# A hybrid decoder block: how its first modulation is loaded and summed, and where the next tokens' transposes stand

## The chip, the cores and the metric

One core of a Trainium2 chip runs the whole kernel in one launch. The metric is the device time of one execution in microseconds (us); less is better. TensorE multiplies matrices, VectorE, ScalarE and GpSimd do element-wise work, SyncE (SP) only issues transfers; each engine takes its instructions in the order of its own queue, and semaphores hold an instruction until what it needs is there.

## The reference

One transformer block over 2048 tokens of width 1024, in float32. Only the parts near the change are shown; the two mixers (a gated linear attention with four heads and a differential attention with four heads), the output projection and the squared-ReLU MLP follow.

```
ada = silu(c) @ ada_w + ada_b                 # c: (1, 1024), ada_w: (1024, 6 * 1024)
sh_a, sc_a, gt_a, sh_m, sc_m, gt_m = split(ada, 6)
h = rms_norm(x, pre_norm_mix) * (1 + sc_a) + sh_a
proj = h @ w_in                               # gla q, k, v, gate rank 16, out gate; diff q, k, v
g_log = log_sigmoid(g_lr @ gate_w + gate_b) / 16
y = concat(gla heads, diff heads) @ w_out
x = x + gt_a * rms_norm(y, post_norm_mix)
...                                           # the MLP, with sh_m, sc_m, gt_m
```

## The kernel before

Tokens go in four groups of 512 (`t` = 0 to 3); a contraction over 1024 is eight steps `k` of 128. Every float32 product is three products of a high and a low part (fp32r): high x high, high x low, low x high. The code is written with a framework that sets the order of each engine's queue itself, from priorities in the order of the program and from a model of when operands, buffers and PSUM banks are ready; so an instruction written later can stand earlier in a queue.

*The start.* `ada_cols(j)` (lines 352 to 370) forms one 1024-wide part of `ada`: eight blocks of ada_w (128 x 1024 each, 512 KB) are loaded into three buffers of tag `wraw`, VectorE multiplies each by a column of silu(c) and adds it to `acc`, and eight products with a column of ones sum `acc` over the partitions into columns. It is done for part 1 (the scale `sc_a`) and then for part 0 (the shift `sh_a`); `load_consts` stands after the first three blocks, and the loads of the first 512 tokens of x after three blocks of the shift. All of these transfers are issued by SP. The buffers `wraw` also hold the raw projection weights.

*A group of tokens.* `load_norm` (line 132) loads four tiles of x, ScalarE squares and sums them, and each is scaled by its inverse root. `modulate` (line 150) then takes eight steps: four transposes on TensorE (L155), scale and shift on ScalarE (L157), the high part on VectorE (L158), the low part on VectorE and GpSimd in turn (L160). The results `hThi`, `hTlo` have two buffers each.

*The gate.* `gate_scan` (line 507) multiplies the tokens by the rank-16 weights (16 products `lrps`, L513 and L514), copies the result out (L516), and for each half `j` makes one product with gate_w (`zps`, L519), an activation chain on ScalarE and a running sum on VectorE. `gates(t)` (line 531) turns this into the decay factors.

*The projections.* `gla_proj` (line 542) takes the weight blocks 2 and 3 with `proj_n` (tokens on the partitions, two PSUM banks of 48 products for each group of tokens, copied out at L553), then 4, 5, 0 and 1 with `proj_t`. The products `lrps`, `zps` and the projections share two PSUM banks of tag "A", the transposes of `modulate` two of tag "C". `gates(0)` is written before `gla_proj`; in it, `norm_in(1)` and `gates(1)` are written between the two groups of the first weight block. For groups 2 and 3, `norm_in(2)` and `gates(2)` are written among the last projections of the groups before, and the same call follows.

*The output projection.* `out_proj` (line 858) goes through the tiles of 128 tokens: it loads the mixed tile `mx` (1 MB, two buffers, in two pieces for the last four tiles) from DRAM, loads x, makes two banks of 24 products each (L873 to L875), and adds the normed result to x. It is a generator: `interleave` (line 945) runs its steps between those of the attention. A tile can only be taken when all heads of its tokens are finished.

Of the kernel before, what the change touches and what calls it, by code (L numbers as in the profile page):

```python
# [14 lines left out]
ALU = mybir.AluOpType  # L15
# [34 lines left out]
def tile_hybrid_block(  # L50
# [48 lines left out]
    def load_consts():  # L99
        nc.sync.dma_start(cols, ada_b)  # L100
        nc.sync.dma_start(prem[:, 0, :], pre_mix)
        nc.sync.dma_start(prem[:, 1, :], pre_mlp)
        nc.sync.dma_start(postm[:, 0, :], post_mix)
        nc.sync.dma_start(postm[:, 1, :], post_mlp)
        nc.sync.dma_start(gnc[:, 0:1], gla_norm)
        nc.sync.dma_start(gnc[:, 1:2], diff_norm)
        nc.sync.dma_start(gbc, gate_b)
        nc.sync.dma_start(ivf, inv_freq)
        nc.sync.dma_start(gw2[0:16], gate_w)
        nc.sync.dma_start(gw2[16:32], gate_w)  # L110
        nc.sync.dma_start(lamt, lams.partition_broadcast(P))

# [19 lines left out]
    def load_norm(src, xp, slots, on_act=False):  # L132

        xts = []
        ss = xp.tile([P, 4], F32, tag="nss", name="nss", bufs=2)
        for i in range(4):
            xt = xp.tile([P, D], F32, tag=slots[i][0], name="nx", bufs=slots[i][1])
            nc.sync.dma_start(xt, src[i])
            junk = xp.tile([P, D], BF16, tag="njunk", name="njunk", bufs=1)
            nc.scalar.activation(junk, xt, AF.Square, accum_out=ss[:, i:i + 1])  # L140
            xts.append(xt)
        r = rsqrt_col(xp, ss, 4, 1.0 / D, "nr")
        for i in range(4):
            if on_act:
                nc.scalar.activation(xts[i], xts[i], AF.Copy, scale=r[:, i:i + 1])
            else:
                nc.vector.tensor_scalar(xts[i], xts[i], r[:, i:i + 1], None, op0=ALU.mult)
        return xts

    def modulate(xts, a1, sh, hi, lo, tp, ttag, tb, pp, ptags):  # L150

        for k in range(NK):
            ps = pp.tile([P, 512], F32, tag=ptags[k % len(ptags)], name="ntr", bufs=2)
            for i in range(4):
                nc.tensor.transpose(ps[:, i * P:(i + 1) * P], xts[i][:, k * P:(k + 1) * P], ident)  # L155
            hf = tp.tile([P, 512], F32, tag=ttag, name="nhf", bufs=tb)
            nc.scalar.activation(hf, ps, AF.Identity, bias=sh[:, k:k + 1], scale=a1[:, k:k + 1])  # L157
            nc.vector.tensor_copy(hi[:, k, :], hf)  # L158
            eng = nc.gpsimd if k % 2 else nc.vector
            eng.tensor_tensor(lo[:, k, :], hf, hi[:, k, :].bitcast(F32), op=ALU.subtract)  # L160


# [148 lines left out]
    def ps_proj(name):  # L311
        return pp.tile([P, 512], F32, tag="A", name=name, bufs=2)
# [96 lines left out]

    def norm_in(t, xts=None, ptags="C"):  # L410
        hi = sb.tile([P, NK, 512], F32R, tag="hThi", name="hThi", bufs=2)
        lo = sb.tile([P, NK, 512], F32R, tag="hTlo", name="hTlo", bufs=2)
        xts = xts or load_x(t)
        modulate(xts, prem[:, 0, :], cols[:, 0:NK], hi, lo, sb, "tA", 8, pp, ptags)
        hT[t] = (hi, lo)

    def split_w(p, pool, nb, eng=nc.vector):
# [11 lines left out]

    sc_a = ada_cols(1)  # L430
    run(sc_a, 3)
    load_consts()
    run(sc_a)
    make_a1(0, 1)
    sh_a = ada_cols(0, sb.tile([P, 4, 256], F32, tag="whi", name="adacc", bufs=3).rearrange("p a b -> p (a b)"))
    run(sh_a, 3)
    xts = load_x(0)
    run(sh_a)
    norm_in(0, xts, "CBDCBDCB")

# [51 lines left out]

    def proj_n(w, t, i2):

        ps = ps_proj("projn")
        whi, wlo = w
        hi, lo = hT[t]
        for i in range(2):
            o = ps[:, i * 256:(i + 1) * 256]
            tk = slice((2 * i2 + i) * P, (2 * i2 + i + 1) * P)  # L500
            for k in range(NK):
                nc.tensor.matmul(o, hi[:, k, tk], whi[k], start=(k == 0), stop=False)  # L502
                nc.tensor.matmul(o, hi[:, k, tk], wlo[k], start=False, stop=False)  # L503
                nc.tensor.matmul(o, lo[:, k, tk], whi[k], start=False, stop=(k == NK - 1))
        return ps

    def gate_scan(t, consts, pool, ta):

        hi, lo = hT[t]
        lw1, lw2, rst = consts[0:3]  # L510
        ps = ps_proj("lrps")
# [3 lines left out]
        lrT = pool.tile([32, 512], F32, tag="lrT", name="lrT", bufs=1)  # L515
        nc.vector.tensor_copy(lrT, ps[0:32, :])  # L516
        for j in range(2):
            zp = ps_proj("zps")
# [11 lines left out]

    def gates(t):
        for j, b16 in gate_scan(t, glac, sg, tA):

# [7 lines left out]

    def gla_proj(ts2):
        for q in range(2):
            w = load_w(2 + q)
            run(rope, 1)
            for t in ts2:
                if q == 0 and t % 2:
                    norm_in(t)
                    gates(t)
                for i2 in range(2):  # L550
                    ps = proj_n(w, t, i2)
                    ev = tA("gvev", F32, (P, 2, 256))
                    nc.scalar.copy(ev.rearrange("p a b -> p (a b)"), ps)  # L553
                    nc.gpsimd.dma_start(gvS[t][:, 2 * i2:2 * i2 + 2, 256 * q:256 * q + 256], ev)
# [101 lines left out]
    def gla_any(tq, gn, gcon, masks):  # L656
# [8 lines left out]
        xts = load_norm([x[tq * 512 + i * P:tq * 512 + (i + 1) * P, :] for i in range(4)], gn, [("nx", 4)] * 4)  # L665
        modulate(xts, prem[:, 0, :], cols[:, 0:NK], hi, lo, gn, "nhf", 2, pp, "C")
        hT[tq] = (hi, lo)
        b16s = [b for _, b in gate_scan(tq, gcon, gn, ta)]
        qr, kr = [], []
# [115 lines left out]

    gates(0)
    gla_proj((0, 1))
    dp, ga = diff_proj((0, 1)), gla((0, 1))
# [3 lines left out]

    norm_in(2)
    run(dp, 1)
    gates(2)
    run(dp)
    run(ga)
    gla_proj((2, 3))
    dp, ga = diff_proj((2, 3)), gla((2, 3))
# [58 lines left out]
    def out_proj(tiles):  # L858

        for tk in tiles:  # L860
            assert all((tk // 4, h) in finished for h in range(NH))
            mx = sw.tile([P, 2 * NH, 2, P], F32R, tag="mx", name="mx", bufs=2)
            for ks in (slice(0, 7), slice(7, 8)) if tk >= 12 else (slice(0, 8),):
                nc.sync.dma_start(mx[:, ks].bitcast(F32), mixS[tk // 4][:, tk % 4, ks])
            xt = sw.tile([P, D], F32, tag="wx", name="wxt", bufs=3)
            nc.sync.dma_start(xt, x[tk * P:(tk + 1) * P, :])
            yps = []
            ss = sw.tile([P, 2], F32, tag="wss", name="wss", bufs=2)
            for b in range(2):
# [631 lines left out]
```

## Time and profile before

| | |
|---|---|
| time, median of 3 runs | 2626.18 us (2623.98 to 2628.01) |
| the profiled execution: its time, its span | 2620.44 us, 2618.7 us |
| TensorE busy | 2482.6 us, 95% of the span |
| VectorE, ScalarE, GpSimd busy | 1595.4, 1154.8, 435.5 us |
| mean granted TensorE clock | 0.982 of full speed |
| mean DMA rate | 188 GB/s |

The span runs from the first to the last instruction of one profiled execution. Busy shares are means over stages with different limits: what a stage can gain is read from its own stretch and from which wait ends last there. Matmuls are pipelined, so the time from one start to the next says more of their price than the duration of one.

### The profile page before, as it was taken

Reading aid. Unit: us, or ns where it says so; the run is one execution under the profiler, and the core shown is the slowest. Engines: PE = TensorE matmul, PEld = TensorE weight load, DVE = VectorE, ACT = ScalarE, POOL = GpSimd, SP = SyncE. Lnnn points to the kernel's source line nnn. Section 1 sums busy time; section 2 is a strip of 40 time slices with the busy share of each in tenths; the row PEclk is TensorE's granted clock in tenths of the full one; section 3 lists DMA queues with packets and bytes.
Section 4 is the critical chain, followed back from the end, with each engine's and each line's share of the span. In section 5 each row is a group of like instructions: output and inputs, shape, how many; then the busy total and the mean of one; then the engine's idle time right before and its main releaser. Section 6 shows DMA issues by size and latency. Waiting matters only on the chain.

```text
span 2618.7 us, 35437 instructions
## 1 busy us (share of the span) xinstructions
PE 2482.6 (95%) x12532; PEld 2043.2 (78%) x12532; DVE 1595.4 (61%) x3111; ACT 1154.8 (44%) x2185; POOL 435.5 (17%) x642
## 2 busy tenths in 40 slices
PE   3999999999998899999999999999999999999998
PEld 2887787987787787787877878788888888788886
DVE  5545765247764766766568666866665435443756
ACT  3351224323444655565546454655454324222444
POOL 1211332102320113223002231121121000100000
PEclk9999999999999899999999999999999999999999
DMA  6354552344744756565376564654447857755856
GB/s 235 107 193 137 170 196 77 125 131 155 224 155 142 227 173 207 186 201 187 109 261 234 194 238 141 225 190 144 139 151 258 289 189 234 268 197 162 282 168 208
DMA packets 219898, 491.63 MB, mean 188 GB/s; under 512 B 25872, under 2 KB 79936, under 8 KB 218176
## 3 DMA queue, kind: packets, MB, share of 16 engines
q1 hardware_dynamic: 171504, 329.33, 39.8%
q0 software_dynamic: 48208, 159.95, 16.3%
q8 instruction: 101, 1.65, 0.3%
q14 instruction: 85, 0.70, 0.1%
HBM read 329.79 MB, written 159.39 MB: 187 GB/s over the span
## 4 chain that ended last, share of the span: by engine, by line
PE 33%; issue 20%; DMA 5%; POOL 5%; DVE 3%; ACT 2%; SPq 0%; POOLq 0%; DVEq 0%; ACTq 0%
PE dn L1361 6%; PE dn L1363 6%; PE dn L1362 6%; PE O L252 3%; PE S L209 3%; PE Y L873 1%; PE Y L875 1%; POOL uS L1121 1%; PE Y L874 1%; POOL uS L1152 1%; PE PT L248 1%; DMA mx<-mixS 1%; PE upY L1195 1%; PE upY L1194 1%; PE upY L1193 1%
## 5 line engine op out<-in xcount | busy, mean ns | idle before, releaser
L1361 PE MATMUL dn<-dnhi,uhi 128*128 128x512 f32 x880 | 344.2, 391 | 4.8 <-DVE du L1339 4.7
L1363 PE MATMUL dn<-dnhi,ulo 128*128 128x512 f32 x880 | 343.8, 391 | 0.1
L1362 PE MATMUL dn<-dnlo,uhi 128*128 128x512 f32 x880 | 343.8, 391 | 0.0
L1285 ACT CAST uhi<-us 128x1024 fp32r<-128x1024 f32 (+1 forms) x126 | 118.7, 944 | 352.6 <-PE dn L1362 325.8
L1287 DVE TENSOR_TENSOR ulo<-us,uhi 128x1024 fp32r<-128x1024 f32 (+1 forms) x126 | 137.0, 1087 | 152.6 <-ACT uhi L1285 149.9
L209 PE MATMUL S<-K,q 128*128 128x512 f32 (+3 forms) x640 | 193.9, 402 | 14.2 <-DVE P L214 7.5
L488 PE MATMUL projt<-hThi,whi 128*128 128x512 f32 x512 | 206.3, 403 | 0.6 <-DVE cols L370 0.3
L489 PE MATMUL projt<-hTlo,whi 128*128 128x512 f32 x512 | 205.9, 402 | 0.0
L490 PE MATMUL projt<-hThi,wlo 128*128 128x512 f32 x512 | 201.8, 394 | 2.1 <-DVE wlo L425 2.1
L1361 PEld LDWEIGHTS dn<-dnhi,uhi 128*128 128x128 f32 x880 | 165.7, 188 | 41.0 <-issue 5.1
L1363 PEld LDWEIGHTS dn<-dnhi,ulo 128*128 128x128 f32 x880 | 165.7, 188 | 35.7 <-DVE ulo L1287 0.6
L1362 PEld LDWEIGHTS dn<-dnlo,uhi 128*128 128x128 f32 x880 | 165.7, 188 | 35.1
L227 ACT ACTIVATE P<-P,nm 128x128 f32<-128x128 f32 (+15 forms) x128 | 153.8, 1203 | 65.2 <-DVE nm L217 59.7
L1075 ACT CAST wuhi<-wA 128x512 fp32r<-128x512 f32 x160 | 99.1, 619 | 162.7 <-PE upV L1194 67.2
L252 PEld LDWEIGHTS O<-V,PTs 128*128 128x128 f32 x1088 | 136.5, 193 | 33.4 <-ACT PTs L250 26.6
L252 PE MATMUL O<-V,PTs 128*128 128x128 f32 x1088 | 154.7, 285 | 7.3 <-ACT PTs L250 3.5
L1195 PE MATMUL upY<-hhi,wulo 128*128 128x512 f32 x384 | 151.0, 393 | 1.5 <-DVE wulo L1076 1.5
L1193 PE MATMUL upY<-hhi,wuhi 128*128 128x512 f32 x384 | 150.9, 393 | 0.0
L1194 PE MATMUL upY<-hlo,wuhi 128*128 128x512 f32 x384 | 150.9, 393 | 0.0
L502 PE MATMUL projn<-whi,hThi 128*128 128x256 f32 x512 | 147.2, 288 | 3.8 <-DVE cols L370 2.3
L209 PEld LDWEIGHTS S<-K,q 128*128 128x128 f32 x640 | 111.7, 197 | 48.8 <-DVE P L214 21.9
L503 PE MATMUL projn<-wlo,hThi 128*128 128x256 f32 x512 | 146.7, 287 | 0.0
(321 smaller groups left out, 5759.9 us busy)
## 6 DMA issues: line engine op xcount, KB each, us to landing
us<-uS SPq DMA_DIRECT2D x94, 512.0 KB, 4.5
wA<-in_w_up_dram SPq DMA_DIRECT2D x128, 256.0 KB, 3.0
uS<-t POOLq DMA_DIRECT2D x128, 256.0 KB, 3.2
adaraw<-in_ada_w_dram SPq DMA_DIRECT2D x48, 512.0 KB, 4.4
wraw<-in_w_in_dram SPq DMA_DIRECT2D x48, 512.0 KB, 4.5
uS<-c POOLq DMA_DIRECT2D x96, 256.0 KB, 3.0
K<-kS SPq DMA_DIRECT2D x40, 512.0 KB, 4.6
wds<-in_w_down_dram SPq DMA_DIRECT2D x78, 256.0 KB, 4.3
```

The source lines that it names most:

```text
L209: nc.tensor.matmul(ps[:, :wd], qt[:, m, hl, qs], Kc[ci][:, m, :wd], start=(hl == 0), stop=(hl == 1))
L227: nc.scalar.activation(Ps[m][:, :width], Ps[m][:, :width], AF.Exp, scale=-1.0, bias=nms[m][:, t:t + 1], accum_out=sums[:, 0, m:m + 1])
L252: nc.tensor.matmul(outs[t, h][:, j, :], pt[:, kb % 4, :], Vc[g][:, kb % 4, :], start=(kb == 0), stop=(kb == nb - 1))
L488: nc.tensor.matmul(ps, whi[k][:, cs], hi[:, k, :], start=(k == 0), stop=False)
L489: nc.tensor.matmul(ps, whi[k][:, cs], lo[:, k, :], start=False, stop=False)
L490: nc.tensor.matmul(ps, wlo[k][:, cs], hi[:, k, :], start=False, stop=(k == NK - 1))
L1193: nc.tensor.matmul(ps, whi[:, k, :], hi[:, k, :], start=(first and k == 0), stop=False, skip_group_check=not first)
L1194: nc.tensor.matmul(ps, whi[:, k, :], lo[:, k, :], start=False, stop=False, skip_group_check=not first)
L1195: nc.tensor.matmul(ps, wlo[:, k, :], hi[:, k, :], start=False, stop=(k == 3), skip_group_check=not first)
L1361: nc.tensor.matmul(banks[t], uhi[:, tk], whi, start=first, stop=False, skip_group_check=on)
L1362: nc.tensor.matmul(banks[t], uhi[:, tk], wlo, start=False, stop=False, skip_group_check=on)
L1363: nc.tensor.matmul(banks[t], ulo[:, tk], whi, start=False, stop=last, skip_group_check=on)
```

## The change

The twelve constant loads are issued by GpSimd and no longer by SP. The eight blocks of the scale and the eight of the shift are loaded whole, into the buffers of `hThi` and `hTlo`, with the four x tiles of the first tokens between them. The scale is summed as before; the shift is summed by TensorE alone, 64 products of 128 x 128 by one column that accumulate in one bank. `norm_rows` is split from `load_norm`. `modulate` becomes a generator: after the first weight block's four k steps each, `proj_n` runs one step of it, so that the transposes of group t + 1 stand among the projection products of group t (for even t). `gate_scan` is split: the rank product (`gate_rank`) stands where the gates stood, and the rest follows the first projection bank. In `out_proj` the next mixed tile's load is written after the first k step of a tile's second bank, if that tile's heads are finished.

```diff
     def load_consts():
-        nc.sync.dma_start(cols, ada_b)
...
-        nc.sync.dma_start(lamt, lams.partition_broadcast(P))
+        nc.gpsimd.dma_start(cols, ada_b)
...
+        nc.gpsimd.dma_start(lamt, lams.partition_broadcast(P))
     def load_norm(src, xp, slots, on_act=False):
         xts = []
-        ss = xp.tile([P, 4], F32, tag="nss", name="nss", bufs=2)
         for i in range(4):
             xt = xp.tile([P, D], F32, tag=slots[i][0], name="nx", bufs=slots[i][1])
             nc.sync.dma_start(xt, src[i])
+            xts.append(xt)
+        return norm_rows(xts, xp, on_act)
...
     def modulate(xts, a1, sh, hi, lo, tp, ttag, tb, pp, ptags):
...
             eng.tensor_tensor(lo[:, k, :], hf, hi[:, k, :].bitcast(F32), op=ALU.subtract)
+            yield
...
     def norm_in(t, xts=None, ptags="C"):
...
-        modulate(xts, prem[:, 0, :], cols[:, 0:NK], hi, lo, sb, "tA", 8, pp, ptags)
         hT[t] = (hi, lo)
+        yield from modulate(xts, prem[:, 0, :], cols[:, 0:NK], hi, lo, sb, "tA", 8, pp, ptags)
...
-    sc_a = ada_cols(1)
-    run(sc_a, 3)
+    def ada_stage(j):
+
+        raw = []
+        for tag in ("hThi", "hTlo"):
+            st = sb.tile([P, NK, 512], F32, tag=tag, name="adast", bufs=2).rearrange("p (r a) b -> p r (a b)", a=2)
+            for r in range(4):
+                k = len(raw)
+                nc.sync.dma_start(st[:, r, :], ada_w[k * P:(k + 1) * P, j * D:(j + 1) * D])
+                raw.append(st[:, r, :])
+        return raw
+
+
     load_consts()
-    run(sc_a)
+    sc_raw = ada_stage(1)
+    x0 = [sg.tile([P, D], F32, tag="nx", name="nx", bufs=4) for _ in range(4)]
+    for i in range(4):
+        nc.sync.dma_start(x0[i], x[i * P:(i + 1) * P, :])
+    sh_raw = ada_stage(0)
+    acc = sb.tile([P, D], F32, tag="adacc", name="adacc", bufs=1)
+    for k in range(NK):
+        if k == 0:
+            nc.vector.tensor_scalar(acc, sc_raw[0], ca[:, 0:1], None, op0=ALU.mult)
+        else:
+            nc.vector.scalar_tensor_tensor(acc, sc_raw[k], ca[:, k:k + 1], acc, op0=ALU.mult, op1=ALU.add)
+    ps = ps_proj("adaps")
+    for b in range(NK):
+        nc.tensor.matmul(ps[:, b:b + 1], acc[:, b * P:(b + 1) * P], ones[:, 0:1], start=True, stop=True)
+    nc.vector.tensor_tensor(cols[:, NK:2 * NK], cols[:, NK:2 * NK], ps[:, 0:NK], op=ALU.add)
     make_a1(0, 1)
-    sh_a = ada_cols(0, sb.tile([P, 4, 256], F32, tag="whi", name="adacc", bufs=3).rearrange("p a b -> p (a b)"))
-    run(sh_a, 3)
-    xts = load_x(0)
-    run(sh_a)
-    norm_in(0, xts, "CBDCBDCB")
+    xts = norm_rows(x0, sg, True)
+    ps = ps_proj("adaps")
+    for k in range(NK):
+        for b in range(NK):
+            nc.tensor.matmul(ps[:, b:b + 1], sh_raw[k][:, b * P:(b + 1) * P], ca[:, k:k + 1], start=(k + b == 0),
+                             stop=(k == NK - 1), skip_group_check=True)
+    nc.vector.tensor_tensor(cols[:, 0:NK], cols[:, 0:NK], ps[:, 0:NK], op=ALU.add)
+    run(norm_in(0, xts, "CBDCBDCB"))
...
-    def proj_n(w, t, i2):
-
+    def proj_n(w, t, i2, between=()):
+
+        between = iter(between)
...
                 nc.tensor.matmul(o, lo[:, k, tk], whi[k], start=False, stop=(k == NK - 1))
+                if k % 4 == 3:
+                    run(between, 1)
         return ps
 
-    def gate_scan(t, consts, pool, ta):
-
+    def gate_rank(t, consts, pool):
...
         nc.vector.tensor_copy(lrT, ps[0:32, :])
+        return lrT
+
+    def gate_scan(lrT, consts, ta):
+
+        rst = consts[2]
...
-                if q == 0 and t % 2:
-                    norm_in(t)
-                    gates(t)
+                if q == 0 and t % 2 == 0:
+                    ni = norm_in(t + 1)
+                elif q == 0:
+                    lrT = gate_rank(t, glac, sg)
                 for i2 in range(2):
-                    ps = proj_n(w, t, i2)
+                    ps = proj_n(w, t, i2, ni if q == 0 and t % 2 == 0 else ())
+                    if q == 0 and i2 == 0:
+                        gates(t, lrT)
...
-    gates(0)
-    gla_proj((0, 1))
+    gla_proj((0, 1), gate_rank(0, glac, sg))
...
-    norm_in(2)
+    run(norm_in(2))
     run(dp, 1)
-    gates(2)
+    lrT = gate_rank(2, glac, sg)
     run(dp)
     run(ga)
-    gla_proj((2, 3))
+    gla_proj((2, 3), lrT)
...
     def out_proj(tiles):
 
-        for tk in tiles:
+        tiles = list(tiles)
+
+        def load_mx(tk):
...
+            return mx
+
+        mxs = {}
+        for n, tk in enumerate(tiles):
+            mx = mxs.pop(tk) if tk in mxs else load_mx(tk)
...
+                    if (b, k) == (1, 0) and n + 1 < len(tiles) and all((tiles[n + 1] // 4, h) in finished for h in range(NH)):
+                        mxs[tiles[n + 1]] = load_mx(tiles[n + 1])
                     yield
```

## Rows read from the trace of the kernel before

**Rows 1.** The page, busy us, share of the span, instructions.

```profile
PE 2482.6 (95%) x12532; PEld 2043.2 (78%) x12532; DVE 1595.4 (61%) x3111; ACT 1154.8 (44%) x2185; POOL 435.5 (17%) x642
```

**Rows 2.** Timeline of the start: start us, us, engine, line, what [idle before].

```profile
2.67 0.43 SPq L100 DMA_DIRECT2D cols<-in_ada_b_dram  x1
...
5.44 0.75 DVE L359 TENSOR_SCALAR adacc<-adaraw,ca 128x1024 f32<-128x1024 f32 x1 [1.97 <-DMA adaraw<-in_ada_w_dram]
...
16.04 3.93 DVE L361 SCALAR_TENSOR_TENSOR adacc<-adaraw,ca,adacc 128x1024 f32<-128x1024 f32 x3 [6.33 <-DMA adaraw<-in_ada_w_dram]
...
23.98 3.58 PE L369 MATMUL adaps<-ones,adacc 128*128 128x1 f32 x16 [23.98 <-DVE adacc L361]
...
39.58 5.24 PE L155 MATMUL ntr<-ident,nx 128*128 128x128 f32 x24 [12.03 <-ACT nx L145]
...
46.20 2.09 PE L369 MATMUL adaps<-ones,adacc 128*128 128x1 f32 x16 [1.38 <-DVE adacc L361]
...
48.53 5.46 ACT L157 ACTIVATE nhf<-ntr,cols,prem 128x512 f32<-128x512 f32 x8 [5.97 <-DVE cols L370]
...
60.92 0.68 DVE L516 COPY lrT<-lrps 32x512 f32<-32x512 f32 x1 [1.43 <-PE lrps L514]
...
65.36 0.58 PE L502 MATMUL projn<-whi,hThi 128*128 128x256 f32 x1
```

**Rows 3.** Stretches: us, busy us (instructions) of each engine, granted clock, DMA share, GB/s.

```profile
61.00:65.30 4.30, 3.65 (x4) 1.16 (x4) 2.70 (x5) 1.48 (x2) 0.00 (x0) 0.56 0.56 181
...
85.10:97.00 11.90, 6.75 (x18) 2.48 (x18) 3.85 (x8) 2.61 (x5) 7.24 (x4) 0.86 0.01 1
...
97.00:104.00 7.00, 7.00 (x58) 7.00 (x59) 5.39 (x9) 4.57 (x8) 0.00 (x0) 1.00 0.12 37
...
438.20:462.00 23.80, 19.16 (x96) 12.67 (x96) 15.72 (x25) 12.85 (x20) 6.08 (x5) 0.86 0.08 29
```

**Rows 4.** Timeline of ScalarE and GpSimd near the first weight block's end.

```profile
108.80 0.59 ACT L553 COPY gvev<-projn 128x512 f32<-128x512 f32 x1 [0.39 <-PE projn L504]
...
104.92 0.72 POOL L554 DMA_DIRECT2D gvS<-gvev  x1 [12.58 <-ACT gvev L553]
```

**Rows 5.** DMA rates of the first 120 us in 40 slices.

```profile
GB/s 30 317 193 35 228 317 227 320 209 296 419 419 228 224 258 283 236 395 182 0 175 168 20 168 261 175 120 57 5 0 0 0 0 87 0 87 16 266 190 221
```

**Rows 6.** Timeline of TensorE: later column sums.

```profile
229.22 1.84 PE L369 MATMUL adaps<-ones,adacc 128*128 128x1 f32 x16
```

**Rows 7.** Timeline around the third and fourth token groups.

```profile
413.61 0.40 PE L513 MATMUL lrps<-hThi,lw 128*32 128x512 f32 x1
...
417.32 1.03 PE L155 MATMUL ntr<-ident,nx 128*128 128x128 f32 x8
...
418.34 1.95 PE L519 MATMUL zps<-lrT,gw 32*128 32x512 f32 x4
...
421.00 0.39 PE L502 MATMUL projn<-whi,hThi 128*128 128x256 f32 x1 [0.71 <-DVE zm L522]
...
438.27 0.58 ACT L553 COPY gvev<-projn 128x512 f32<-128x512 f32 x1 [5.03 <-PE projn L504]
...
461.90 0.59 ACT L553 COPY gvev<-projn 128x512 f32<-128x512 f32 x1
```

**Rows 8.** Timeline and SP's waits (us, times, longest) at the mixed tiles.

```profile
851.09 0.77 PE L873 MATMUL Y<-wohi,mx 128*128 128x512 f32 x1 [7.14 <-DMA mx<-mixS]
...
1322.68 0.60 ACT L878 ACTIVATE wjunk<-Y 128x512 bf16<-128x512 f32 x1 [4.93 <-PE Y L875]
...
1323.36 4.65 SPq L864 DMA_DIRECT2D mx<-mixS  x4
...
1331.44 0.77 PE L873 MATMUL Y<-wohi,mx 128*128 128x512 f32 x1 [4.26 <-DMA mx<-mixS]
...
1334.14 0.63 PE L873 MATMUL Y<-wohi,mx 128*128 128x512 f32 x1
...
SPq L864 <- PE Y L875: 26.2, 3, 22.6
```

More of the change, by code (lines that the diff above doesn't have):

```diff
@@ L99, in load_consts @@
     def load_consts():
-        nc.sync.dma_start(cols, ada_b)
[L101 to L110, printed above, removed]
-        nc.sync.dma_start(lamt, lams.partition_broadcast(P))
+        nc.gpsimd.dma_start(cols, ada_b)
+        nc.gpsimd.dma_start(prem[:, 0, :], pre_mix)
+        nc.gpsimd.dma_start(prem[:, 1, :], pre_mlp)
+        nc.gpsimd.dma_start(postm[:, 0, :], post_mix)
+        nc.gpsimd.dma_start(postm[:, 1, :], post_mlp)
+        nc.gpsimd.dma_start(gnc[:, 0:1], gla_norm)
+        nc.gpsimd.dma_start(gnc[:, 1:2], diff_norm)
+        nc.gpsimd.dma_start(gbc, gate_b)
+        nc.gpsimd.dma_start(ivf, inv_freq)
+        nc.gpsimd.dma_start(gw2[0:16], gate_w)
+        nc.gpsimd.dma_start(gw2[16:32], gate_w)
+        nc.gpsimd.dma_start(lamt, lams.partition_broadcast(P))
     neglam = const.tile([P, 1], F32, name="neglam")
@@ L138, in load_norm, with norm_rows @@
             nc.sync.dma_start(xt, src[i])
+            xts.append(xt)
+        return norm_rows(xts, xp, on_act)
+    def norm_rows(xts, xp, on_act):
+        ss = xp.tile([P, 4], F32, tag="nss", name="nss", bufs=2)
+        for i, xt in enumerate(xts):
             junk = xp.tile([P, D], BF16, tag="njunk", name="njunk", bufs=1)
             nc.scalar.activation(junk, xt, AF.Square, accum_out=ss[:, i:i + 1])
-            xts.append(xt)
         r = rsqrt_col(xp, ss, 4, 1.0 / D, "nr")
@@ L504, in proj_n @@
                 nc.tensor.matmul(o, lo[:, k, tk], whi[k], start=False, stop=(k == NK - 1))
+                if k % 4 == 3:
+                    run(between, 1)
         return ps
-    def gate_scan(t, consts, pool, ta):
+    def gate_rank(t, consts, pool):
         hi, lo = hT[t]
-        lw1, lw2, rst = consts[0:3]
+        lw1, lw2 = consts[0:2]
         ps = ps_proj("lrps")
@@ L529, in tile_hybrid_block, with gates @@
     E, Ei = {}, {}
-    def gates(t):
-        for j, b16 in gate_scan(t, glac, sg, tA):
+    def gates(t, lrT):
+        for j, b16 in gate_scan(lrT, glac, tA):
             nc.vector.tensor_scalar(b16, b16, MIN_LOG16, None, op0=ALU.max)
@@ L540, in gates, with gla_proj @@
             E[t, j], Ei[t, j] = e1, e2
-    def gla_proj(ts2):
+    def gla_proj(ts2, lrT):
         for q in range(2):
@@ L665, in gla_any @@
         xts = load_norm([x[tq * 512 + i * P:tq * 512 + (i + 1) * P, :] for i in range(4)], gn, [("nx", 4)] * 4)
-        modulate(xts, prem[:, 0, :], cols[:, 0:NK], hi, lo, gn, "nhf", 2, pp, "C")
+        run(modulate(xts, prem[:, 0, :], cols[:, 0:NK], hi, lo, gn, "nhf", 2, pp, "C"))
         hT[tq] = (hi, lo)
-        b16s = [b for _, b in gate_scan(tq, gcon, gn, ta)]
+        b16s = [b for _, b in gate_scan(gate_rank(tq, gcon, gn), gcon, ta)]
         qr, kr = [], []
```

## The prediction

> **What bounds the kernel now.** I read the page's busy times first: TensorE is busy 95% of the span [rows 1]. So only two things can shorten this kernel: stretches in which TensorE has nothing to do, and stretches in which it runs at its low clock. The table of 50 us stretches shows where they are: the first 100 us, the attention part (some us in each stretch, from many small waits), and the place at 1330 us where the output projection ends. I then read the first stage by smaller stretches and by the timeline. The reader is to see four things there. SP issues twelve small constant loads before it goes on with ada_w, and VectorE then waits 6.33 us for the fourth block [rows 2]. The shift's sum is ready only with the second group of column sums at 46.2 us, and the first modulated tile starts at 48.53 [rows 2]. The first projection product starts at 65.36, after the gate products [rows 2]. Between 85.1 and 97 us TensorE is busy 6.75 of 11.9 us, beside GpSimd with 7.24, and it comes back at a granted clock below 1.00 [rows 3]. The same hole stands at 438 to 462 us for the fourth token group: 19.16 busy of 23.8 us, clock 0.86 [rows 3]. From 108.8 us on the first stage is all TensorE, so what that point (the copy of the fourth projection bank of the first weight block [rows 4]) gains, the end gains.
>
> **The change, part by part. Loads.** Twelve constant loads move from SP to GpSimd's queue. An issue there costs 0.72 us [rows 4], so about 9 us of a queue that has no other work then; the first of them (cols) is wanted only when the scale's column sums are done. I cost this at nothing; without that cover (a late cols) it would be a us or two. The 8 scale blocks, 4 x tiles and 8 shift blocks go out in a row. The first block is used at 5.44 [rows 2]. The best slices of the DMA line show 419 GB/s [rows 5], which is 1.25 us for 524 KB, so the eighth block lands near 14.2, the last x tile near 19.2, the first shift block near 20.5, the last near 29.2. VectorE needs about 1.3 us a block and keeps up; the scale is done near 16 instead of 23.9 and its column sums near 19.5.
>
> In a sentence apart: the Trainium skill ("DMA: Bandwidth & Descriptors", Specifications) puts HBM at about 358 GB/s for a core; the trace's slices go above it, and by its figure the first shift block would come some 2.5 us later, an estimate.
>
> **The shift on TensorE.** What was 8 VectorE multiply-adds and 8 products becomes 64 products. The trace shows 16 TensorE instructions for 8 such products, so 128. Their price has two ends: 3.58 us for 16 at the start (0.22 each), and 1.84 us in a dense stretch later (0.115 each) [rows 2, 6]. The twofold step is that of the clock's two levels, 1.2 and 2.4 GHz. So 28.2 us or 14.7 us. Which one? The work is long but each product has one column. The nearest row is the stretch from 61.0 to 65.3: TensorE was busy 3.65 of 4.3 us with the narrow gate products and the granted clock was 0.56 over it [rows 3]; being busy alone did not bring it up. Against that, 24 transposes from 39.58 ran at 0.22 each, and the column sums after them, at 46.2, ran at 0.13 [rows 2]: there it came up. I take the low price, at 60 to 40 or so. It begins at 20.5, when the first block has landed, since 3.58 us for 16 is slower than the 1.25 us in which blocks arrive: TensorE, not the DMA, sets the end. The 24 transposes of the first tokens (5.24 us at the low price) are ready about 27 and lie partly among the 64 products; I put half of them before the end of the sum. So 20.5 + 28.2 + 2.6 + 0.3 for the add = **51.6 us** for the first modulated tile, where it was 48.53; at the high price 20.5 + 14.7 + 1.3 + 0.3 = 36.8. By itself, then, the new sum is likely no gain.
>
> **The gate pulled apart, and transposes among projections.** Before, both PSUM banks of tag A went to the two gate products ahead of the first projection, so nothing could fill the wait for the modulated tiles: 48.53 to 60.92 for the gate's rank product, then 65.36 [rows 2]. Now only the rank product stands there, and the first projection bank has the other buffer; its three products per k can run as each tile comes. The weights were waited for too (they shared their buffers with ada_w); now they are loaded and split before. Counting from the first modulated tile (T): 12.4 us to the rank product's end before; 11.5 without the weight split and the lambda sums in VectorE's way; I take 13 for the rank product and the first projection bank together. Then the gate products: 418.34 to the next projection at 421.00, 2.7 us [rows 7], and 0.6 for a bank that must be copied out first, 3.3. A projection bank is 48 products at 7.00/58 = 0.12 [rows 3], 5.7 us. 32 transposes are 8 for 1.03 us [rows 7], 4.1, and 0.3 for changing over, 4.4. The rank product is 413.61 to 417.32, 3.7 [rows 7]. So T + 13 + 3.3 + 5.7 + 4.4 + (3.7 + 5.7) + 3.3 + 5.7 = T + 44.8. With T = 51.6 that is 96.4 against 108.6 before (0.2 ahead of the copy's start): **-12.2 us**. With T = 36.8 it is 81.6: -27. VectorE has 15.72 us of work for one token group's tiles and gates [rows 3]; only its tiles (some 9 us) are wanted before the rank product of the next, so it fits, but not by much: this is what is late next.
>
> A rule speaks against this. The row: from 39.58 TensorE did nothing but transposes, and what followed ran at nearly the high price [rows 2]. The Trainium skill ("TensorE: Matmul & The Clock Gate", Part 4) says that the full clock is not engaged in transpose mode, since transposes do not count as busy in the same way. The trace does not agree at this place. By the rule the transposes put among the projections could pull the clock down; see the third rival.
>
> **The fourth token group.** Before, 438.27 to 461.90 is 23.6 us [rows 7] for work that costs 5.7 + 4.4 + 3.7 + 3.3 = 17.1: at most 6.5 to win, less 0.6 for the third group's gate products, which only move. VectorE carries the gates and tiles of two groups in about 19 us of TensorE work, so I take half: **-3 us** (0 to -6).
>
> **The next mixed tile ahead.** TensorE waits 4.26 us for mx at 1331.44 and its next products run at the low clock (0.63 us of duration, down to 1334.14), some seven of them, 1.4 us more [rows 8]. But the load had been issued at 1323.36, just after the two sums at 1322.68, and SP's longest waits at this line are for the output products [rows 8]: the two buffers were full, and asking sooner gives no third one. The other wait, 7.14 at 851.09 [rows 8], is for the first tile, which nobody asks for ahead. I take **0** (bounds 0 to -5.7).
>
> **Sum.** -12.2 - 3 + 0 = -15.2 us. The profiled execution took 2620.44 (span 2618.7 and 1.7 around it), which would become 2605.2. The runs shown have a median 0.22% above that one, 2626.18, so the time to expect of runs is **2611.0**. A measurement of this kernel can tell about 0.2%, 5.25 us.
>
> **Rivals.** (1) The clock rises during the shift's products: T = 36.8, sum -27 - 3 = -30, time 2596. For it: the rise after the transposes. Against it: the gate products at 0.56. Chance 0.26. (2) The stage gains nothing to speak of: VectorE or GpSimd hands over the tiles late, as at 85 to 97 us now, or the new order among the queues gives small waits elsewhere; then about -3, time 2623. Chance 0.11. (3) Transposes among projection products lower the clock: 192 products of the two stages at the low level's twofold, 0.24 instead of 0.12 each, cost up to 23 us, half of it where they are among the transposes, 11.5; the gain shrinks to 4, time 2622; with all of it net +8, 2634. Against it stands the row at 39.58. Chance 0.05. (4) The other side: an mx load asked for ahead waits for its buffer at SP's head and holds the K, V and q loads of the attention behind it. SP's waits at this line reach 22.6 us at the end of the attention [rows 8], while those loads are asked for only two steps ahead. One such stall costs what 851.09 shows: 7.14 and some 2.5 at the low clock after it, 9.6 us. From two on the gain is gone, at three the time is 2626 - 15.2 + 28.8 = 2640. Against it: the load is asked for when half of the tile before is done, when the older buffer is already free. Chance 0.08. That leaves 0.50 for the forecast, whose own range is 2603 to 2620 (T between 49 and 54, the fourth group between 0 and -6, mx up to -5.7).
>
> **Numbers.** The range takes in the first rival's time with some us below and reaches up to about no change: 2591 to 2625. Faster by over 0.2%: the forecast and the first rival, 0.76, and a little of the second: 0.78. Within: the second and third, 0.13. Slower: 0.09.
>
> **What would show it.** In the profile after: the scale's products end near 16 us; 128 instructions of the shift's sum from about 20 us at 0.22 (or 0.11) each; the first modulated tile at 52 (or 37); projection products among the first rank products; no hole of 3 us ahead of the second group's; the fourth copy of the first weight block near 96; the wait for the next-to-last mixed tile still there. I am wrong if the sum ends before 45 us, if TensorE's transposes stand in front of it waiting for the x tiles, or if the attention part grows by more than 5 us.

## The result and the profile after

The changed kernel takes 2635.3 us (median of 8 runs, 2631.4 to 2638.2) against 2623.4 us for the kernel before in runs beside it: ratio 1.0046, 95% interval 1.0035 to 1.0057. It is slower by about 12 us. Forecast were 2611.0 us in a range of 2591 to 2625, with 0.78 for faster and 0.09 for slower: the time lies outside the range and the sign was wrong. The profiled execution took 2634.72 us, span 2633.0.

The page's line of busy times of the changed kernel:

```profile
PE 2505.8 (95%) x12644; PEld 2071.8 (79%) x12644; DVE 1585.5 (60%) x3103; ACT 1155.5 (44%) x2185; POOL 439.1 (17%) x654
```

TensorE has 112 instructions more than in [rows 1], the 128 of the shift's sum for the 16 they replace, and is busy 23.2 us longer. Where time is lost is seen in the timeline of the start (start us, us, engine, line, what, and in brackets the idle time before with its releaser):

```profile
17.53 3.57 PE L463 MATMUL adaps<-ones,adacc 128*128 128x1 f32 x16 [17.53 <-DVE adacc L460]
...
22.54 6.99 PE L470 MATMUL adaps<-ca,adast 128*128 128x1 f32 x32 [1.44 <-DMA adast<-in_ada_w_dram]
...
29.39 1.73 PE L160 MATMUL ntr<-ident,nx 128*128 128x128 f32 x7
...
34.19 2.59 PE L160 MATMUL ntr<-ident,nx 128*128 128x128 f32 x11
...
39.84 1.52 PE L160 MATMUL ntr<-ident,nx 128*128 128x128 f32 x6
...
41.16 13.65 PE L470 MATMUL adaps<-ca,adast 128*128 128x1 f32 x64
...
54.85 0.16 DVE L472 TENSOR_TENSOR cols<-cols,adaps 128x8 f32<-128x8 f32 x1 [31.25 <-PE adaps L470]
55.04 5.47 ACT L162 ACTIVATE nhf<-ntr,cols,prem 128x512 f32<-128x512 f32 x8 [27.15 <-DVE cols L472]
...
60.36 2.03 ACT L431 CAST whi<-wraw 128x1024 fp32r<-128x1024 f32 x2
...
64.59 1.21 DVE L432 TENSOR_TENSOR wlo<-wraw,whi 128x1024 fp32r<-128x1024 f32 x1
...
66.98 0.64 PE L550 MATMUL lrps<-hTlo,lw 128*32 128x512 f32 x1 [1.85 <-POOL hTlo L165]
...
67.42 0.41 PE L538 MATMUL projn<-wlo,hThi 128*128 128x256 f32 x1
```

The reader is to see three things. The scale's column sums begin 6.4 us sooner than in [rows 2]: the loads work. Then TensorE has no gap from 22.54 to 54.8, with 32 instructions in 6.99 us, 64 in 13.65, and all 24 transposes among them. And ScalarE stands idle 27.15 us until 55.04, with VectorE behind the same sum for 31.25 us; the casts of the first projection weights, although those were loaded early, follow only at 60.36, their low halves at 64.59, and the projection runs in earnest from 67.42. The first modulated tile is 6.5 us later than before (48.53 in [rows 2]).

The second place is behind the first projection bank. Its last product starts at 77.89 (the first line of this timeline):

```profile
77.89 0.28 PE L539 MATMUL projn<-whi,hTlo 128*128 128x256 f32 x1
...
82.03 0.69 ACT L562 ACTIVATE za<-zps,gbc 128x512 f32<-128x512 f32 x1
...
84.83 1.12 PE L560 MATMUL zps<-lrT,gw 32*128 32x512 f32 x2 [1.98 <-DVE zm L563]
...
88.02 0.58 PE L537 MATMUL projn<-whi,hThi 128*128 128x256 f32 x1 [2.08 <-DVE zm L563]
...
89.40 0.56 ACT L597 COPY gvev<-projn 128x512 f32<-128x512 f32 x1
...
96.76 0.47 PE L549 MATMUL lrps<-hThi,lw 128*32 128x512 f32 x1
...
112.24 0.58 PE L537 MATMUL projn<-whi,hThi 128*128 128x256 f32 x1 [2.20 <-DVE zm L563]
...
120.26 0.59 ACT L597 COPY gvev<-projn 128x512 f32<-128x512 f32 x1 [0.36 <-PE projn L539]
```

The bank is full at 78, and ScalarE copies it at 89.40: the copy is written behind the gate chain (L562 to L579) in ScalarE's order. For 11 us one of the two banks of tag A holds finished sums, and the second gate product (84.83) and the second projection bank (88.02) must take turns on the other. The same happens four times, at t = 0 to 3. TensorE's waits (us in total, times, longest) say so:

```profile
PE Y L923 <- DMA mx<-mixS: 11.8, 3, 7.2
PE projn L537 <- DVE zm L563: 8.0, 4, 2.2
...
PE zps L560 <- DVE zm L563: 6.9, 4, 2.0
...
PE lrps L550 <- POOL hTlo L165: 3.9, 3, 1.9
```

The same waits in the kernel before:

```profile
PE lrps L514 <- POOL hTlo L160: 9.5, 8, 3.6
...
PE projn L502 <- DVE zm L522: 1.5, 2, 0.8
```

The waits for zm (the gate's minimum, which frees a gate product's bank) were 1.5 us in all before and are 14.9 now; the waits of the rank products for GpSimd fell from 9.5 to 3.9. The fourth copy of the first weight block comes at 120.26, against 108.80 in [rows 4]; the last copy of the second stage at 501.00 against 490.76.

At the mixed tiles little moved. The first still waits 7.22 us, the next-to-last 2.61 instead of 4.26 [rows 8]; what is new is one wait in the down projection, in the timeline of TensorE:

```profile
859.43 0.77 PE L923 MATMUL Y<-wohi,mx 128*128 128x512 f32 x1 [7.22 <-DMA mx<-mixS]
...
1341.18 0.47 PE L923 MATMUL Y<-wohi,mx 128*128 128x512 f32 x1 [2.61 <-DMA mx<-mixS]
...
2073.68 0.50 PE L1415 MATMUL dn<-dnhi,ulo 128*128 128x512 f32 x1 [2.86 <-DVE ulo L1339]
```

### The profile page after: what moved, and what is told of

It is laid out like the page before. It is cut to its first block, busy times and chain, and to the rows that moved or that the text cites. A ratio compares the mean times of both kernels' runs of the same rounds, so it can differ in the third digit from the quotient of the medians.

```text
span 2633.0 us, 35644 instructions
## 1 busy us (share of the span) xinstructions
PE 2505.8 (95%) x12644; PEld 2071.8 (79%) x12644; DVE 1585.5 (60%) x3103; ACT 1155.5 (44%) x2185; POOL 439.1 (17%) x654
## 4 chain that ended last, share of the span: by engine, by line
PE 38%; issue 19%; DMA 4%; POOL 3%; DVE 2%; ACT 2%; SPq 0%; POOLq 0%; DVEq 0%; ACTq 0%
PE dn L1413 4%; PE dn L1415 4%; PE dn L1414 4%; PE upY L1247 3%; PE upY L1245 3%; PE upY L1246 3%; PE O L258 2%; PE S L215 2%; PE upX L1247 2%; PE upV L1245 2%; PE upV L1246 2%; PE upV L1247 2%; PE upX L1245 2%; PE upX L1246 2%; PE PT L254 1%
## 5 line engine op out<-in xcount | busy, mean ns | idle before, releaser
L233 ACT ACTIVATE P<-P,nm 128x128 f32<-128x128 f32 (+15 forms) x128 | 153.8, 1203 | 65.2 <-DVE nm L223 64.5
L539 PE MATMUL projn<-whi,hTlo 128*128 128x256 f32 x512 | 149.7, 292 | 0.0
```

Of the source, the lines that this page charges most:

```text
L233: nc.scalar.activation(Ps[m][:, :width], Ps[m][:, :width], AF.Exp, scale=-1.0, bias=nms[m][:, t:t + 1], accum_out=sums[:, 0, m:m + 1])
```

## The experiments

Every kernel computes the whole reference. "Us against before" is the difference of medians with the kernel before run in the same series; the ratio's interval stands beside it. Two kernels are compared by these differences. **Theory A**: two losses that add, the shift's sum on TensorE and the gate chain ahead of the copy. **Rival B**: all of it lies in the gates and the transposes among projections. **Rival C**: the earlier loads of mixed tiles cost the attention.

**The three parts one by one.** d1_start is the changed kernel with gates, transposes and mixed tiles as before; d2_gates keeps only those gates and transposes; d3_mx only the loads of mixed tiles. In d1_start and d3_mx:

```diff
-                if q == 0 and t % 2 == 0:
-                    ni = norm_in(t + 1)
-                elif q == 0:
-                    lrT = gate_rank(t, glac, sg)
+                if q == 0 and t % 2:
+                    run(norm_in(t))
+                    gates(t)
...
```

and in d1_start and d2_gates the prefetch is left out (the two lines with `mxs[tiles[n + 1]]`), in d2_gates and d3_mx the start is that of the kernel before.

> The start part alone: constants issued by GpSimd, both ada_w blocks and the first tokens loaded at once, the shift summed by 128 one-column products; gates, transposes of the next tokens and mixed tiles as in the kernel before. Theory A (the shift on TensorE holds back the first modulated tile, and everything in order behind it): first modulated tile at 55 us as in the changed kernel against 48.5 before, and the end 5 to 9 us later than before. Rival B (the whole loss lies in the gates and transposes; what the start loses is given back at the first weight block): end 0 to 3 us earlier than before, or no later. Rival C (the mixed tiles): no difference from before.

> The gates and transposes alone: gate products behind the first projection bank, transposes of tokens t+1 among the projection products of tokens t; start and mixed tiles as before. Theory A: the hole at the low-rank products of t=1 and 3 goes away, but the copy of the first projection bank stands behind the gate chain on ScalarE, four times, with low clock after; net 2 to 6 us slower than before. Rival B (all of the loss is here): 10 to 14 us slower. Rival C: 0 to 3 us faster, since a hole is gone.

> The earlier loads of the mixed tiles alone. Theory A and rival B: within 1.5 us of before, the waits for mixed tiles still 11 to 12 us in sum. Rival C (the loads stand ahead of K, V and q loads on SyncE's queue, and the attention pays): 4 us or more slower.

Measured: d1_start 2631.44 us, +9.2 (1.0027 to 1.0053); d2_gates 2627.93 us, +5.7 (1.0010 to 1.0040); d3_mx 2620.65 us, -1.6 (0.9990 to 1.0017). The sum, +13.3, is the +12 of the whole within its uncertainty, so the parts hardly meet each other. Rival C is out, and so is B: more than half of the loss is the start. In d1_start the first modulated tile stood at 55.60. In the profiled execution of d2_gates it stood at 50.56, 2.0 us later than before although its start is the old one: there the 16 column sums took 3.57 us and not 2.09. So up to 2 of its 5.7 us may not belong to the gates.

**The shift on VectorE.** d4_dve sums the same staged blocks as the scale is summed:

```diff
-    for k in range(NK):
-        for b in range(NK):
-            nc.tensor.matmul(ps[:, b:b + 1], sh_raw[k][:, b * P:(b + 1) * P], ca[:, k:k + 1], start=(k + b == 0),
-                             stop=(k == NK - 1), skip_group_check=True)
...
+    for k in range(NK):
...
+            nc.vector.scalar_tensor_tensor(acc, sh_raw[k], ca[:, k:k + 1], acc, op0=ALU.mult, op1=ALU.add)
+    for b in range(NK):
+        nc.tensor.matmul(ps[:, b:b + 1], acc[:, b * P:(b + 1) * P], ones[:, 0:1], start=True, stop=True)
```

> The changed kernel with the shift summed by VectorE from the same staged blocks (8 products with a column of the activation, accumulated in SBUF, then 8 one-column products with ones, as for the scale), all else as changed. Theory A: first modulated tile at 37 to 42 us instead of 55, and the end 10 to 16 us earlier than the changed kernel, so about level with the kernel before or up to 5 us under it. Rival B: the first modulated tile earlier as well, but the end within 3 us of the changed kernel. Rival C: as A for the start, but at least 4 us of the loss stay behind the attention.

Measured: 2612.28 us, -9.9 (0.9946 to 0.9975), 22 us less than the changed kernel. Its timeline:

```profile
23.79 9.25 DVE L472 SCALAR_TENSOR_TENSOR adacc<-adast,ca,adacc 128x1024 f32<-128x1024 f32 x7
...
33.09 3.04 PE L475 MATMUL adaps<-ones,adacc 128*128 128x1 f32 x16 [2.60 <-DVE adacc L472]
...
36.37 5.46 ACT L162 ACTIVATE nhf<-ntr,cols,prem 128x512 f32<-128x512 f32 x8 [8.32 <-DVE cols L476]
```

The first modulated tile starts at 36.37, 18.7 us sooner than with the products. The blocks and their loads are the same; the engine that sums them is the whole difference. It is more than theory A had (10 to 16 us).

**Half and half.** k1_half lets TensorE take blocks 0 to 3 and VectorE 4 to 7, and adds VectorE's sum with 8 products with ones in the same bank:

```diff
-    for k in range(NK):
+    for k in range(4):
         for b in range(NK):
             nc.tensor.matmul(ps[:, b:b + 1], sh_raw[k][:, b * P:(b + 1) * P], ca[:, k:k + 1], start=(k + b == 0),
-                             stop=(k == NK - 1), skip_group_check=True)
+                             stop=False, skip_group_check=True)
...
```

> The changed kernel with the shift shared: TensorE takes blocks 0 to 3 as one-column products (64 instead of 128 instructions), VectorE sums blocks 4 to 7 at the same time, and 8 products with ones add its sum in the same bank. Theory A (the first modulated tile waits for the products at 0.215 us each, and what it is late is paid nearly one for one at the end): first modulated tile at 43 to 48 us, the end about half way between d4_dve and the changed kernel, from 4 us under to 4 us over the kernel before. Rival (the loss is one of the clock, all or nothing): as d4_dve (8 to 12 us under) or as the changed kernel (9 or more over).

Measured: 2619.58 us, -3.1 (0.9983 to 1.0006), first modulated tile at 44.98. From d4_dve the tile is 8.6 us later and the end 6.8; from d4_dve to the changed kernel 18.7 and 21.8. So what the first tile is late is paid at the end about one for one, and the three kernels give no sign of a threshold; the two halves, 6.8 and 15.0 us, are each uncertain by some 4 us.

**The start alone, done in that way.** e2_dvestart is d1_start with d4_dve's sum.

> The start part alone, with the shift on VectorE; gates, transposes and mixed tiles as in the kernel before. Theory A: first modulated tile at 36 us, the fourth copy of the first weight block at 96 to 100 us (108.8 before), 13 to 18 us under the kernel before, that is, 3 to 8 us faster than d4_dve. Rival (the gate part costs nothing once the first tile is early): 8 to 12 us under the kernel before, as d4_dve.

Measured: 2607.19 us, -14.2 (0.9930 to 0.9963), first tile at 36.02, fourth copy at 98.91. So loading both blocks at once is worth 14 us, and the products took 23 us (2631.44 less 2622.22, plus 14.2).

**The order on ScalarE.** e1_late is d4_dve, g1_late the changed kernel itself, each with one move:

```diff
-                    if q == 0 and i2 == 0:
-                        gates(t, lrT)
                     ev = tA("gvev", F32, (P, 2, 256))
                     nc.scalar.copy(ev.rearrange("p a b -> p (a b)"), ps)
+                    if q == 0 and i2 == 0:
+                        gates(t, lrT)
```

> As d4_dve (shift on VectorE, 10 us under the kernel before), with one move: the two gate products and their chain are written behind ScalarE's copy of the first projection bank instead of ahead of it. Theory A (the copy queued behind the gate chain keeps a bank of the pair occupied, PE waits 8.5 + 6.9 us for the minimum of the gate and runs at the lower clock after): the waits of PE for zm fall by at least half, the low-clock stretches shorten, 13 to 18 us under the kernel before. Rival B (the transposes among the projection products are what costs): no change from d4_dve, 8 to 12 us under the kernel before.

> The changed kernel, shift on TensorE as changed, with the one move of e1_late alone: the gate products and their chain written behind ScalarE's copy of the first projection bank. Theory A (two separate losses that add: about 23 us between the shift on TensorE and on VectorE, about 17 us by the place of the gate chain): 15 to 20 us faster than the changed kernel, so 2 to 8 us under the kernel before. Rival (the two losses overlap, since both hold ScalarE's queue at the start): less than 8 us faster than the changed kernel, 4 us or more over the kernel before.

Measured: e1_late 2594.98 us, -26.4 (0.9881 to 0.9921), 16.5 us less than d4_dve; g1_late 2617.11 us, -5.6 (0.9965 to 0.9986), 17.4 us less than the changed kernel. e1_late gained more than was expected, g1_late what was. The move is worth the same with either sum: the two losses add. In e1_late's timeline the copy comes 4.4 us after the bank is full (its last product starts at 58.80), behind four modulated tiles and no longer behind the gate chain, and the next bank starts 3 us after the copy; in the changed kernel copy and next bank come 11 and 10 us after the bank is full:

```profile
58.80 0.28 PE L543 MATMUL projn<-whi,hTlo 128*128 128x256 f32 x1
...
60.53 3.03 ACT L162 ACTIVATE nhf<-ntr,cols,prem 128x512 f32<-128x512 f32 x4 [7.69 <-PE ntr L160]
...
63.46 0.58 ACT L599 COPY gvev<-projn 128x512 f32<-128x512 f32 x1
...
64.21 1.12 PE L564 MATMUL zps<-lrT,gw 32*128 32x512 f32 x2
...
66.25 0.39 PE L541 MATMUL projn<-whi,hThi 128*128 128x256 f32 x1 [0.92 <-DVE zm L567]
```

g1_late starts its first tile at 55.13, the changed kernel at 55.04, so their stretches can be laid side by side (us, busy us of PE, PEld, DVE, ACT, POOL with instructions, granted clock, DMA share, GB/s). The changed kernel:

```profile
67.00:75.00 8.00, 8.00 (x28) 6.18 (x29) 7.21 (x16) 3.92 (x9) 0.00 (x0) 0.50 0.39 129
75.00:85.00 10.00, 6.92 (x49) 5.64 (x48) 9.60 (x17) 4.83 (x7) 2.08 (x2) 0.96 0.48 158
85.00:95.00 10.00, 7.92 (x43) 7.09 (x44) 7.22 (x12) 6.16 (x10) 2.51 (x3) 0.66 0.07 26
95.00:105.00 10.00, 10.00 (x73) 8.11 (x72) 2.23 (x4) 2.03 (x3) 1.98 (x2) 1.00 0.08 28
105.00:115.00 10.00, 6.23 (x29) 4.44 (x28) 5.97 (x9) 5.70 (x9) 0.52 (x1) 0.75 0.09 26
```

g1_late:

```profile
75.00:85.00 10.00, 7.64 (x48) 5.22 (x47) 9.62 (x15) 5.83 (x9) 2.98 (x3) 0.99 0.53 184
85.00:95.00 10.00, 10.00 (x66) 8.89 (x66) 8.83 (x15) 7.07 (x12) 2.04 (x3) 0.84 0.00 0
95.00:105.00 10.00, 9.41 (x60) 6.93 (x58) 1.08 (x2) 1.75 (x3) 2.35 (x3) 1.00 0.08 28
105.00:115.00 10.00, 9.60 (x69) 9.60 (x70) 6.96 (x12) 7.48 (x12) 0.72 (x1) 0.83 0.18 56
```

Over these 40 us TensorE is busy 31.07 us (194 instructions) in the changed kernel and 36.65 (243) in g1_late, and in the two stretches with the waits the granted clock is 0.66 and 0.75 against 0.84 and 0.83. By the eighth copy the move has gained 7.8 us (142.92 to 135.17), by the end of the second stage 14.9 (501.00 to 486.09).

**Banks or queue.** n1_aheadD is d4_dve (chain ahead of the copy) with the gate products in banks of their own:

```diff
-            zp = ps_proj("zps")
+            zp = pp.tile([P, 512], F32, tag=ztag, name="zps", bufs=2)
...
-        for j, b16 in gate_scan(lrT, glac, tA):
+        for j, b16 in gate_scan(lrT, glac, tA, "D"):
```

> As d4_dve (chain ahead of the copy), but the gate products write into the banks of tag D, so they need no bank of the pair that the projections use. If the shared banks are the cause: the waits for zm (15.4 us in d4_dve) go away and the time is that of e1_late, 22 to 28 us under the kernel before. If the place in ScalarE's queue is the cause: the third projection bank still waits for the copy behind the chain, the waits are named differently but stay, and the time is near d4_dve, 8 to 14 us under the kernel before. Between the two if both count.

Measured: 2598.20 us, -22.8 (0.9894 to 0.9930), 13 us less than d4_dve. The waits for zm are gone, and one wait of another name is left of them:

```profile
PE lrps L553 <- ACT gvev L601: 5.6, 1, 5.6
```

So the loss needs both the late copy and the two banks that gate products, rank products and projections share: taking either away gives back most of the 17 us, 16.5 by the copy's place and 13 by the banks. With banks of its own for the gate, the copy's late place costs 2.4 us (e3_lateD below, which differs from n1_aheadD in that alone), which these runs do not tell from nothing.

**Both, and the transposes.** e3_lateD has the chain behind the copy and the banks of tag D; e4_blocktr is e3_lateD with the transposes in one block again (`run(norm_in(t))` ahead of `gate_rank`).

> As e1_late, and the gate products write into the PSUM banks of tag D (idle in this stage) instead of the pair that the projections use. Theory A: no wait of PE for zm at all, the copies of the projection banks free their banks at once, no hole at the low-rank products of tokens 1 and 3: 16 to 22 us under the kernel before. Rival B (transposes among the products): not more than 12 us under it.

> As e3_lateD, but the 32 transposes of tokens 1 and 3 stand in one block ahead of their low-rank products, as in the kernel before, instead of among the projection products. Theory A: the hole is back (waits of the low-rank products for GpSimd some 5 to 6 us more, twice two tiles), 4 to 9 us slower than e3_lateD. Rival B (among the products they cost what they hide): within 2 us of e3_lateD, or faster.

Measured: e3_lateD 2596.21 us, -25.2 (0.9882 to 0.9922), no better than e1_late. e4_blocktr 2600.57 us, -20.8 (0.9901 to 0.9936): 4.4 us slower. The intervals of the two overlap, but each of the five times of e4_blocktr lies above each of the four of e3_lateD. The hole at the second group's rank products is back in part, in e4_blocktr's timeline:

```profile
80.17 0.42 PE L554 MATMUL lrps<-hTlo,lw 128*32 128x512 f32 x1 [1.04 <-POOL hTlo L165]
...
82.42 0.42 PE L554 MATMUL lrps<-hTlo,lw 128*32 128x512 f32 x1 [0.82 <-POOL hTlo L165]
```

The transposes among the products are thus a gain of some 4 us, and rival B falls a second time.

**Further back.** h1_second puts the chain behind the second copy (`i2 == 1`), h2_deferred does so for the even token group and puts the odd one's behind the first copy of the second weight block.

> As e1_late, with the gate products and chain behind the second copy of a token tile instead of the first. Theory A (what stands in ScalarE's queue between a bank's end and its copy sets the loss): the remaining waits of PE for zm (3.3 us) fall or move, 0 to 6 us faster than e1_late, 26 to 32 us under the kernel before. Rival (the chain then collides with the next tokens' modulated tiles on ScalarE and VectorE, and the low-rank products wait longer): 2 to 8 us slower than e1_late.

> As h1_second for the even token tile; the gate chain of the odd one stands behind the first copy of the second weight block, where all waits for modulated tiles are over. Theory A: the chain no longer meets anything that PE waits for, 2 to 8 us faster than e1_late. Rival: no gain over e1_late within 2 us, since the odd tile's chain met nothing there either.

Measured: h1_second 2594.23 us, -28.4 (0.9872 to 0.9911); h2_deferred 2599.94 us, -22.7 (0.9900 to 0.9933). h1_second is level with e1_late (2.0 us, within the uncertainty). h2_deferred is not faster than e1_late but 3.7 us slower, which is no more than the uncertainty of the two; theory A had 2 to 8 us faster. Its waits of projection products for zm grew to 5.4 us (2 times), at 100.09 and 451.03, right behind the second block's first bank: there the odd chain's gate products take a bank of the pair again. Kernels e1_late and h1_second are faster than both the kernel before and the changed one, by 1.0% and about 1.5%.

## Why the prediction was wrong

**The balance**, from medians: loads with VectorE's sum -14 (e2_dvestart); that sum on TensorE +22 (21.8, 20.8 and 23.4 in the three pairs); gates pulled apart and transposes among the products, with the copy ahead of the gate chain, -12 (e1_late less e2_dvestart, the mixed tiles in it); the chain ahead of the copy +17. Together +13, where +12 was measured. Steps along one path from the kernel before to the changed one have to add up to it; that the two losses add is shown by each having the same size with the other and without it (21.8 and 20.8, 16.5 and 17.4). Two good ideas, 26 us, were each spent by a detail of its own.

**Loads: right, and undervalued.** The scale's products ended at 17.47 (forecast near 16), and the first shift block was there at 22.54 (20.5). The DMA moved 370 GB/s from 4 to 14 us and 406 or 407 after it, somewhat below the 419 of [rows 5]. In a sentence apart: the figure that the prediction cited from the Trainium skill ("DMA: Bandwidth & Descriptors", Specifications), about 358 GB/s, gave 23.0 for that block, half a microsecond off, but the rates after it lie well above that figure.

**The shift's price: right; its place in the sum too small.** 128 instructions ran at 0.213 to 0.218 each, the low price, so the first rival did not happen. T came at 55.04, not 51.6: the first block 2.0 later, and all 24 transposes inside the sum (5.2 us, half had been put there), less 1.2 for products that took 27.0 us and not 28.2. That step called the new sum by itself "likely no gain". It was compared with the old start, and not with the same loads summed by VectorE, which d4_dve shows at T = 36.4 (T is again the start of the first modulated tile).

**T + 44.8 is the step that failed.** It was T + 65.2, in these terms: rank product and first bank 13, measured 23.0; gate products, second bank and transposes 13.4, measured 18.7 (to 96.76); rank product 3.7, measured 3.8; third bank and gates 9.0, measured 11.7 (to 112.24); fourth bank 5.7, measured 8.0. Two assumptions are behind that. First, "now they are loaded and split before": loaded, yes, but the casts stand in ScalarE's queue behind the eight modulated tiles (60.36, and 41.68 in d4_dve, T + 5.3 both times), and they stood at T + 5.3 in the kernel before as well:

```profile
53.84 2.03 ACT L424 CAST whi<-wraw 128x1024 fp32r<-128x1024 f32 x2
```

So nothing was won there. The rank product alone ended at 67.62, T + 12.6, where it had ended at T + 12.4; only one product of the first bank stood ahead of its last one (66.98), and the others came behind it, at a granted clock of 0.50 until 75 us and with a gate product (70.11, 2.07 us) among them. The forecast had put both into 13 us. This is the largest part of the miss, 10.0 us; that the place of the casts causes all of it is argued from the order and not shown, since no run moved them. Second, a single price of 3.3 us for the gate products, with "0.6 for a bank that must be copied out first": the 0.6 is the copy's length, and its place in ScalarE's order was not looked up. With the copy in front (g1_late) the stage is T + 58.3, so 6.9 of the 20.4 us missed are the order. T + 44.8 was reached in no version: h2_deferred (89.54, T + 51.9) and h1_second (89.26, T + 52.3) come nearest, and they only move the chain behind that copy: in h1_second the fifth copy is at 102.88, in e1_late at 100.36. The second rival named small waits from the new order among the queues, but priced them at no gain and not at a loss.

**The fourth group, -3 forecast, was a loss.** From the first copy of the V projection (376.61 before, 383.58 after) to the last copy of the second stage the lag grows from 7.0 to 10.2 us: +3.2. The hole did go (the rank products of t = 3 run from 454.57 at 0.23 a piece without a wait, as those of t = 1 do from 96.76), and the same two waits per group for zm came in its place.

**The mixed tiles: right.** 0 forecast, -1.6 measured, within the uncertainty; the fourth rival did not occur. None of the three signs by which the prediction would have called itself wrong came either: they were a sum that ends early, transposes that wait in front of it and a longer attention, and what happened was a sum that ended late and a longer first weight block.

**Transposes and the clock: right.** In e3_lateD TensorE is busy all of the stretch from 56.6 to 66.6 us, with 24 transposes among some 50 projection products, at a granted clock of 1.00:

```profile
56.60:66.60 10.00, 10.00 (x75) 8.75 (x75) 8.23 (x14) 4.87 (x8) 2.05 (x2) 1.00 0.37 128
```

That the third rival's full case, 2634 us, lies near the measured time is chance: with the transposes taken out again (e4_blocktr) the kernel is slower. In a sentence apart: the rule of the Trainium skill ("TensorE: Matmul & The Clock Gate", Part 4) that transposes do not engage the full clock does not show in this stretch, where they are mixed with products. Another place of the same page ("A second HAM failure mode: psum-queue depth-cycling") does bear on this case, and the trace agrees: it says of a kernel which cycles through PSUM banks that TensorE idles for a moment between groups so often that its clock goes back and forth between its levels; here the waits for a bank stand in stretches with a granted clock of 0.66 and 0.75.

**What stays open.** The last 3 to 4 us of the profiled difference arise in the down projection (the wait of 2.86 us above); such waits differ from kernel to kernel and no run was made on them. That the low price of the one-column products is the clock's is read from their durations alone, and the granted-clock column speaks against it (last section). The DMA is not what slows them: from 41 to 54.8 us it moved nothing, and the price was the same as before, 0.213. Nor did any run show why 16 column sums took 2.09 us in the kernel before and 3.57 in d2_gates at the same place.

## What to carry to other kernels

When work moves to an engine, compare it with the same loads summed where they were summed before, not only with the old schedule: otherwise a gain of one half of the change hides the loss of the other. When a product is put between two others, look up which buffers it shares with them and where the instruction that frees each buffer stands in its engine's order; here a 0.6 us copy that stood some 11 us late behind a chain cost 17 us over four places. Write the copy that frees a bank ahead of anything that does not feed TensorE next.

## What the runs showed of the hardware that was not expected

TensorE was busy for 31.96 of the 32.0 us from 22.5 to 54.5 with one-column products and transposes, and its instructions kept the low price to the last: 64 of them took 13.65 us at the end (0.213 each) and 16 take 1.84 us in a dense stretch [rows 6] (0.115 each). A busy engine is thus not yet a fast one. The granted-clock column of that stretch (the third number from the end) reads 1.00 all the while:

```profile
22.50:54.50 32.00, 31.96 (x152) 31.96 (x152) 0.63 (x4) 4.74 (x6) 0.00 (x0) 1.00 0.47 187
```

So in this stretch the column alone would have hidden a price nearly twice the one in the dense stretch: where column and durations disagree, read both.
